# Expert groups recorded as a pipeline, a scatter in two f32r passes, another chain of norms into block 2, a new load price in the plan and an announced branch

## The chip, the core and the metric

The kernel runs on one core of a Trainium2 chip. The metric is the time of one execution on the device in microseconds; the median of three runs is given, and one more execution was taken with the hardware profiler.

## What is computed

Two transformer blocks on 256 tokens of width 1024, all in float32. The first has two kinds of attention and a mixture of experts; the second has two layers, each with a mixer, an attention into 256 memory tokens and a gated feed-forward layer. The change is about the experts and about the passage from the first block to the second:

```python
def hierarchical_moe(h, ...):          # 4 groups x 8 experts, top 2 in the chosen group
    ...
    weight = p_group * softmax(top_vals)
    ...
    def expert_block(args):
        xb, e = args
        return (silu(xb @ w_g[e]) * (xb @ w_u[e])) @ w_d[e]
    ...
    out = zeros((T, D)).at[slot_tok].add(ys * slot_w[:, None])
...
    x = x + hierarchical_moe(rmsnorm(x, ffn_norm), ...)
    return rmsnorm(x, final_norm)      # end of the first block
...
    h = rmsnorm_2(x, norm_mix[0])      # start of the second block
```

There are 32 experts with an inner width of 256, so gate and up weights are 64 MB and down weights 32 MB, all of which are read.

## The kernel before, in words

**Order of the work.** The kernel doesn't issue instructions directly. A `Recorder` (line 164) takes every operation with its tiles; `plan` (line 290) then runs a list schedule over five engines: `price` (line 191) gives each operation a cost, an operation is ready when those it depends on are done and its tiles have a buffer, and of the ready ones an engine takes that with the lowest number (recording order less `bias`). `run` (line 434) then issues everything in the order found, from the one line 461, so nearly all rows name L461. Every engine executes its own instructions strictly in that order. Loads stay in the order of recording on SP's queue; one of 1 MB is priced at 2915 ns (line 221).

**Buffers.** A load of expert weights (`raw`, line 533) is a tile of 8 KB in each partition and takes any free buffer of four shared rings: `w`, `h` and `l` with three each and `n8` with six, less those that operations recorded earlier still need. A slab (`slab`, line 539) for a product in three passes needs one of `w`, `h` and `l`: after the load ACT rounds it to f32r (`h`) and VectorE takes the remainder (`l`), in two halves. A product of two matrices is then three f32r passes, `h` with the high and low part of the other side and `l` with its high part (`mm3`, line 560). Temporary tiles are in the rings `ta` and `tb`, PSUM banks in the rings `pg` (3), `pa` (2), `pb` (2) and `pm` (1).

**The experts' stage** (`moe`, line 1028). Tokens are sorted into 32 slots of each expert by a selection matrix `st`. The loop from line 1048 runs over eight groups of four experts. At each even group the gather (`ga`) of eight experts makes `xs` from f32r parts of x; `cs` is the transposed selection with the routing weights, `rs` the row scale. Each group then has 32 products `gu` (four f32 products of 32 columns side by side, eight loads `w_gu`), the activation `act`, its transposition `at`, 16 products `by` (four loads `w_dn`, in the order first half, second half, first half, second half), two copies `y` on ACT, eight f32 scatter products `co` and four sums into x on VectorE. Then come `MEM_EVERY[g]` steps of the memory (line 1132): 18 steps in all (`memory`, line 1255) make the keys and values of the second block's memory attention, each with one slab `w_xkv` and 48 f32r products `fm` or `tm`. They hold TensorE's time within the stage. One step is in the first block's attention, two run during the routing, 14 in the loop, and one is left and comes behind `two_norms` (line 1554).

Before group 7 two slabs of the second block are recorded, `w_eqk[0]` and `w_ev[0]` (line 1050).

**The branch.** An expert with more than 32 tokens needs more work. It stands behind `tc.If(late > 0)` (line 1149, `moe_late`) and is not taken with these inputs, so each engine jumps over it. The jump comes behind group 1 (`LATEG`), where the plan puts a barrier: only loads are planned across it.

**Into block 2** (`two_norms`, line 1201). Two norms follow one another. The mean of x squared gives `r` by a chain of logarithm, exponential and one Newton step (`rsq`, line 603); a second mean, with the gain, gives `rbc` by a second such chain from the first. The products of the second block take x with both gains before the norm and are multiplied by `rbc` afterwards, so they need not wait for it; `even_mixer` (line 1341) begins with them.

Of the kernel before, what the change touches and what calls it, by code (L numbers as in the profile page):

```python
# [10 lines left out]
F32 = mybir.dt.float32  # L11
# [19 lines left out]
NEXTG = 7  # L31
NEXT = 2
# [5 lines left out]
MEM_EVERY = (2, 2, 2, 2, 2, 2, 1, 1)  # L38
# [125 lines left out]
class Recorder:  # L164
# [5 lines left out]
    TABLE = 1300.0  # L170
    FIRST = "natural_log_exp_and_others"

    def __init__(self, tc, pools):
        self.tc, self.nc, self.pools = tc, tc.nc, pools
        self.count, self.starts, self.bufs, self.ops, self.bars = {}, {}, {}, [], []
        for n in ("tensor", "vector", "scalar", "gpsimd", "sync"):
            setattr(self, n, Engine(self, n))
        self.bias = 0

# [11 lines left out]
    def price(self, engine, method, a, k):  # L191
# [29 lines left out]
        return 2915.0 * n / 2048 if engine == "sync" else 100  # L221
# [212 lines left out]
    def run(self):  # L434
# [13 lines left out]
        for idx, nxt in zip(order, after):  # L448
# [9 lines left out]
    def issue(self, op):  # L458
        r = lambda v: v.real() if isinstance(v, View) else v
        for method, a, k in op.calls:  # L460
            getattr(getattr(self.nc, op.engine), method)(*map(r, a), **{n: r(v) for n, v in k.items()})  # L461


class Net:
# [32 lines left out]
    def consts(self):  # L497
# [25 lines left out]
        self.ones = cp.tile([128, 5, 128], F32, name="ones")  # L523
        for i, v in enumerate((1.0 / 1024, 1.0 / 256, 1.0 / 128, -1.0, 1.0)):
            nc.gpsimd.memset(self.ones[:, i, :], v)
        self.k1024, self.k256, self.k128, self.kneg, self.kone = (self.ones[:, i, :] for i in range(5))
# [3 lines left out]
        for i in range(8):  # L530
            nc.gpsimd.memset(self.order[:, i:i + 1], float(8 - i))

# [70 lines left out]
    def rsq(self, p, out, ms, n, mul=1.0):  # L603
# [4 lines left out]
        nc.scalar.activation(u, ms, AF.Ln, bias=self.eps)  # L608
        nc.scalar.activation(u, u, AF.Exp, scale=-0.5)
        nc.vector.tensor_tensor(t, u, u, ALU.mult)  # L610
        nc.vector.scalar_tensor_tensor(t, ms, EPS, t, ALU.add, ALU.mult)
# [173 lines left out]
    def block1_attention(self, steps):  # L785
# [18 lines left out]
        for i, ac in enumerate(accs):  # L804
            for t in range(2):
                for hf in range(2):
                    o = T * hf + 128 * t
                    self.mm(bs[:, 2 * i + t:2 * i + t + 1], ac[:, o:o + 128], self.kone[:, 0:1], hf == 0, hf == 1)
# [139 lines left out]
    def route(self, rtm):  # L948
# [14 lines left out]
        small = lambda name, *s: self.small(name, 2, *s, bufs=1)  # L963
# [59 lines left out]
        self.mm(b[0:1, 0:1], n, self.kone[:, 0:1])  # L1023
# [4 lines left out]
    def moe(self, steps, early, every):  # L1028
# [17 lines left out]
        slot = self.c("slot")  # L1046
        self.next = []
        for g in range(8):
            if g == NEXTG:
                self.next = [self.slab(w, 256) for w in (a["w_eqk"][0], a["w_ev"][0], a["w_eqk"][1])[:NEXT]]  # L1050
            p, q = divmod(g, 2)
            if q == 0:
                st = self.temp("a", "st", [128, 2, 8, SLOTS], F32R)
                ct, rt = (self.temp("b", n, [128, 2, 8, SLOTS]) for n in ("ct", "rt"))
                for t in range(2):
                    pe = lambda v: v[:, t, 8 * p:8 * p + 8][:, :, None].to_broadcast([128, 8, SLOTS])
                    nc.vector.tensor_tensor(st[:, t], pe(place), slot[:, None, :].to_broadcast([128, 8, SLOTS]),
                                            ALU.is_equal)
                    nc.vector.tensor_tensor(ct[:, t], st[:, t], pe(wt), ALU.mult)
                    nc.vector.tensor_scalar(rt[:, t], st[:, t], rtm[:, t:t + 1], None, ALU.mult)  # L1060
                stv, ctv, rtv = (v.rearrange("p t e s -> p t (e s)") for v in (st, ct, rt))
                xs = self.big("xs", [128, KC, 256])
                for i in range(4):
                    b = self.bank("g", "ga")
                    for j in range(2):
                        c = 2 * i + j
                        for n, (hs, t) in enumerate(((hh, 0), (hl, 0), (hh, 1), (hl, 1))):
                            self.mm(b[:, 256 * j:256 * j + 256], hs[:, t, 128 * c:128 * c + 128], stv[:, t, :],
                                    n == 0, n == 3)
                    for j in range(2):  # L1070
                        c = 2 * i + j
                        gc = self.gcol("ffn_norm", c)
                        if j:
                            nc.scalar.activation(xs[:, c, :], b[:, 256 * j:256 * j + 256], AF.Copy, scale=gc)
                        else:
                            nc.vector.tensor_scalar(xs[:, c, :], b[:, 256 * j:256 * j + 256], gc, None, ALU.mult)
                b = self.bank("m", "cb")
                for i in range(2):
                    for t in range(2):
                        o = 256 * i + 128 * t  # L1080
                        nc.tensor.transpose(b[:, o:o + 128], ctv[:, t, 128 * i:128 * i + 128], self.ident)
                cs = self.temp("b", "cs", [128, 2, T])
                nc.vector.tensor_copy(cs, self.two(b))
                b = self.bank("m", "rs")
                for i in range(2):
                    for t in range(2):
                        self.mm(b[:, i:i + 1], rtv[:, t, 128 * i:128 * i + 128], self.kone[:, 0:1], t == 0, t == 1)
                rs = self.small("rs", 2)
                nc.vector.tensor_copy(rs, b[:, :2])
            bg = self.bank("a", "gu")  # L1090
            for k in range(KC):
                w = self.raw(a["w_gu"][g, k])
                calls = []
                for j in range(4):
                    o = 128 * q + 32 * j
                    calls.append(("matmul", (bg[32 * j:32 * j + 32, :], xs[:, k, o:o + 32],
                                             w[:, 512 * j:512 * j + 512]),
                                  dict(start=k == 0, stop=k == KC - 1, skip_group_check=True)))
                nc.record("tensor", calls)
            act = self.temp("a", "act", [128, 2, 256])  # L1100
            nc.scalar.activation(act[:, 0, :], bg[:, :256], AF.Silu, scale=rs[:, q:q + 1])
            nc.vector.scalar_tensor_tensor(act[:, 0, :], bg[:, 256:], rs[:, q:q + 1], act[:, 0, :],
                                           ALU.mult, ALU.mult)
            b = self.bank("b", "at")
            for i in range(2):
                nc.tensor.transpose(b[:, 128 * i:128 * i + 128], act[:, 0, 128 * i:128 * i + 128], self.ident)
            at = act[:, 1, :]
            nc.vector.tensor_copy(at, b[:, :256])
            by = [self.bank("b", f"by{i}") for i in range(2)]
            for k in range(2):  # L1110
# [579 lines left out]
```

## Time and profile before

| | us |
|---|---|
| median of three runs (1283.58 to 1288.8) | 1283.79 |
| the profiled execution itself | 1278.79 |
| its span in the profile | 1277.0 |
| TensorE busy | 1207.3 |
| VectorE busy | 851.4 |
| ACT busy | 649.5 |

The profile has the busy time of each engine over the whole span and in stretches; TensorE's products are pipelined, so its busy time is not its peak. PE is TensorE, PEld its weight loads, DVE VectorE, ACT ScalarE, POOL GpSimd, SP the queue that issues all loads. An f32 product leaves two records, an f32r product one. The experts' stage lies between about 230 and 515 us.

### The profile page before, as it was taken

What the parts mean: (1) busy time and instruction counts of PE and PEld (TensorE: products, weight loads), DVE (VectorE), ACT (ScalarE), POOL (GpSimd) and SP (SyncE); (2) the same over time, 40 slices, a digit from 0 to 9 for tenths busy, and PEclk for the clock granted to TensorE, in tenths of its full rate; (3) what the DMA queues carried; (4) which work ended last, traced back from release to release, by engine and by line L of the source; (5) the groups of instructions that cost most, each with busy time, mean ns of one, the idle gap of its engine ahead of it and who ended that gap; (6) DMA issues with size and microseconds to landing.
All of it is one profiled execution on the core that took longest, in us unless ns stands there. A gap on an engine that the chain in (4) does not pass through costs nothing.

```text
span 1277.0 us, 22671 instructions
## 1 busy us (share of the span) xinstructions
PE 1207.3 (95%) x9325; PEld 1078.8 (84%) x9325; DVE 851.4 (67%) x1529; ACT 649.5 (51%) x1111; POOL 8.9 (1%) x71
## 2 busy tenths in 40 slices
PE   8999999987878876999999999999999999999998
PEld 7999999555545542898999999999999999999997
DVE  7666677424432242998877977777755687877775
ACT  7664554323322231765545655555766655555543
POOL 1000000000000000000000000000000000000000
PEclk9999999999999998999999999999999999999999
DMA  7623565888999989443441555554433342555541
GB/s 271 238 100 133 214 247 201 340 358 358 392 399 392 420 320 408 164 174 131 167 166 67 198 199 171 193 195 168 166 133 132 106 167 99 192 193 172 185 176 67
DMA packets 40143, 273.55 MB, mean 214 GB/s; under 512 B 4576, under 2 KB 4576, under 8 KB 8032
## 3 DMA queue, kind: packets, MB, share of 16 engines
q1 hardware_dynamic: 40032, 272.03, 57.0%
q8 instruction: 75, 1.23, 0.4%
q14 instruction: 36, 0.29, 0.1%
HBM read 270.96 MB, written 1.05 MB: 213 GB/s over the span
## 4 chain that ended last, share of the span: by engine, by line
PE 67%; DVE 4%; DMA 2%; ACT 2%; issue 1%; SPq 0%; DVEq 0%; ACTq 0%
PE fm L461 41%; PE dn L461 10%; PE tm L461 4%; PE gu L461 2%; DMA w<-w_dn 2%; PE co L461 2%; DVE l L461 2%; PE oz L461 1%; PE by L461 1%; PE mo L461 1%; PE ms L461 1%; PE ga L461 1%; PE hn L461 1%; DMA w<-w_gu 1%; PE bo L461 1%
## 5 line engine op out<-in xcount | busy, mean ns | idle before, releaser
L461 PE MATMUL fm<-xh,h 128*128 128x256 f32 x1824 | 526.9, 290 | 13.9 <-ACT h L461 6.0
L461 PE MATMUL fm<-xh,l 128*128 128x256 f32 x1824 | 518.7, 285 | 6.7 <-DVE l L461 6.7
L461 PE MATMUL fm<-xl,h 128*128 128x256 f32 x1824 | 516.9, 284 | 0.0
L461 DVE TENSOR_TENSOR l<-w,h 128x1024 fp32r<-128x1024 f32 (+2 forms) x328 | 382.9, 1191 | 62.3 <-ACT h L461 61.5
L461 ACT ACTIVATE h<-w 128x1024 fp32r<-128x1024 f32 (+2 forms) x328 | 325.4, 1027 | 178.4 <-issue 86.2
L461 PEld LDWEIGHTS fm<-xh,h 128*128 128x128 f32 x1824 | 350.2, 192 | 18.4 <-ACT h L461 6.9
L461 PEld LDWEIGHTS fm<-xh,l 128*128 128x128 f32 x1824 | 350.5, 192 | 8.3 <-DVE l L461 8.0
L461 PEld LDWEIGHTS fm<-xl,h 128*128 128x128 f32 x1824 | 350.6, 192 | 2.1 <-issue 0.7
L461 PE MATMUL tm<-l,xh 128*128 128x256 f32 (+2 forms) x364 | 104.6, 288 | 3.9 <-DVE l L461 3.9
L461 PE MATMUL tm<-h,xh 128*128 128x256 f32 (+2 forms) x364 | 107.0, 295 | 0.1
L461 PE MATMUL tm<-h,xl 128*128 128x256 f32 (+2 forms) x364 | 104.0, 286 | 0.0
L461 DVE SCALAR_TENSOR_TENSOR fc<-fu,partile,fc 128x256 f32<-128x256 f32 x176 | 73.4, 479 | 1.3 <-ACT fc L461 1.3
L461 PEld LDWEIGHTS tm<-l,xh 128*128 128x128 f32 x364 | 69.6, 191 | 5.2 <-DVE l L461 4.6
L461 PEld LDWEIGHTS tm<-h,xh 128*128 128x128 f32 x364 | 69.4, 191 | 3.0 <-issue 1.3
L461 PE MATMUL gu<-w,xs 128*32 128x512 f32 x512 | 64.9, 623 | 6.3 <-DMA w<-w_gu 6.3
L461 PEld LDWEIGHTS tm<-h,xl 128*128 128x128 f32 x364 | 69.5, 191 | 0.4
L461 PE MATMUL dn<-fa,h 128*128 128x256 f32 x352 | 64.2, 282 | 1.1 <-ACT fa L461 0.6
L461 DVE TENSOR_TENSOR x<-x,co 128x512 f32<-128x512 f32 x32 | 21.8, 687 | 53.6 <-PE co L461 53.6
L461 PE MATMUL dn<-h,fa 128*128 128x512 f32 x176 | 57.0, 396 | 0.0
L461 DVE TENSOR_TENSOR fu<-fm,rbc 128x512 f32<-128x512 f32 x44 | 30.2, 687 | 38.2 <-PE fm L461 38.0
L461 PEld LDWEIGHTS dn<-fa,h 128*128 128x128 f32 x352 | 54.4, 189 | 1.6 <-ACT fa L461 0.8
L461 DVE SCALAR_TENSOR_TENSOR act<-gu,rs,act 128x256 f32<-128x256 f32 x8 | 3.9, 484 | 70.2 <-ACT act L461 70.2
(291 smaller groups left out, 1386.4 us busy)
## 6 DMA issues: line engine op xcount, KB each, us to landing
w<-w_gu SPq DMA_DIRECT2D x64, 1024.0 KB, 8.9
w<-w_up SPq DMA_DIRECT2D x44, 1024.0 KB, 4.9
w<-w_dn SPq DMA_DIRECT2D x32, 1024.0 KB, 9.5
w<-w_down SPq DMA_DIRECT2D x22, 1024.0 KB, 4.9
w<-w_xkv SPq DMA_DIRECT2D x16, 1024.0 KB, 9.6
w<-w_in_d SPq DMA_DIRECT2D x8, 1024.0 KB, 4.8
w<-w_xq SPq DMA_DIRECT2D x8, 1024.0 KB, 4.9
w<-w_xo SPq DMA_DIRECT2D x8, 1024.0 KB, 5.1
```

The lines of the kernel that those rows point to most:

```text
L461: getattr(getattr(self.nc, op.engine), method)(*map(r, a), **{n: r(v) for n, v in k.items()})
```

## The change

- **Pipeline.** The loop is recorded anew: the next group's gate and up products (`gate_up`) stand half behind this group's activation and half behind its first output half; the gather of the next pair (`gather`) stands behind an even group; the output is done in two halves (`expert_out`), each with its own two loads `w_dn`; one memory step stands between the halves, the others at the end. `MEM_EVERY` ends in 0, so 13 steps are in the loop and two are left.
- **Scatter.** The routing weight no longer is in the matrix: `rw` scales the rows of the output, which is split into two f32r parts `yh` and `yl`; the scatter is two f32r passes with the transposed selection `sb` in place of one f32 product.
- **Chain.** `two_norms` sums the squares with and without gain on TensorE and takes `rbc` from both sums in one chain; `r`, for x itself, follows later. `w_eqk[0]` is recorded in group 7 behind all `w_gu`, `w_ev[0]` behind the sums of squares. The two memory steps that are left run behind the products of the first head in `even_mixer`; some keys use other PSUM rings.
- **Plan.** A load of 1 MB is priced at 2480 ns.
- **Branch.** 120 operations ahead of the barrier each engine gets a hint that the jump is likely taken.
- Besides, small tiles are packed: the routing's into one temporary tile, `ones` loses a column block, `ali` uses the ring of `sb`.

```diff
-MEM_EVERY = (2, 2, 2, 2, 2, 2, 1, 1)
+MEM_EVERY = (2, 2, 2, 2, 2, 2, 1, 0)
...
-        return 2915.0 * n / 2048 if engine == "sync" else 100
+        return 2480.0 * n / 2048 if engine == "sync" else 100
...
+        early = [n - self.AHEAD for n, i in enumerate(order) if i < 0]
+        for n, (idx, nxt) in enumerate(zip(order, after)):
+            if n in early:
+                for engine in mybir.ALL_ENGINES:
+                    if engine in self.last:
+                        with tc.issue_after(self.last[engine].ins):
+                            tc.mark_branch_hint_location("late", "LikelyTaken", engines=[engine])
...
+        xs, rest = self.gather(0, hh, hl, place, wt, rtm)
+        banks = [self.bank("a", "gu")]
+        self.gate_up(0, range(KC), xs, banks[0])
         for g in range(8):
...
+            (st, rw), q = rest, g % 2
+            at = self.gated(banks[g], rw, q)
+            if g < 7:
+                if q == 0:
+                    ahead = xs
+                banks.append(self.bank("a", "gu"))
+                self.gate_up(g + 1, range(KC // 2), ahead, banks[g + 1])
+            else:
+                self.next.append(self.slab(a["w_eqk"][0], 256))
+            self.expert_out(g, 0, at, st, rw, q)
+            take = every[g]
+            if take:
+                steps.pop(0)()
+            if g < 7:
+                self.gate_up(g + 1, range(KC // 2, KC), ahead, banks[g + 1])
+            self.expert_out(g, 1, at, st, rw, q)
+            if g % 2 == 0 and g < 6:
+                ahead, later = self.gather(g // 2 + 1, hh, hl, place, wt, rtm)
+            if q:
+                xs = ahead
+                if g < 7:
+                    rest = later
             if g == LATEG:
                 nc.barrier(lambda: self.moe_late(hh, hl, rtm, wlate, flag), [hh, hl, rtm, wlate, flag, x])
-            for _ in range(every[g]):
+            for _ in range(max(0, take - 1)):
                 steps.pop(0)()
...
+    def expert_out(self, g, i, at, sb, rw, q):
...
+        yh, yl = (self.temp(p, n, [128, 512], F32R) for p, n in (("a", "yh"), ("b", "yl")))
+        self.parts(yh, yl, by, rw[:, 2 + q:3 + q])
+        for h in range(2):
+            b = self.bank("g", "co")
+            for j in range(2):
+                s = slice(256 * h + 128 * j, 256 * h + 128 * j + 128)
+                self.mm(b[:, T * j:T * j + T], yh[:, s], sb[:, q, :], True, False)
+                self.mm(b[:, T * j:T * j + T], yl[:, s], sb[:, q, :], False, True)
+            xv = x[:, 4 * i + 2 * h:4 * i + 2 * h + 2, :]
+            nc.vector.tensor_tensor(xv, xv, self.two(b), ALU.add)
...
-        with tc.If(late > 0):
+        with tc.If(late > 0, label="late"):
...
+        acc = self.tile([128, 512], "acc", "acc", 2)
+        b = self.bank("m", "st")
         for i in range(4):
+            sq = self.temp("s", "sq", [128, 512])
             for c in (2 * i, 2 * i + 1):
                 self.parts(xh[:, c, :], xl[:, c, :], x[:, c, :], gg[:, c:c + 1])
...
+            nc.scalar.activation(sq, self.pair(x, i), AF.Square)
             for j in range(2):
...
+                self.mm(b[:, :T], self.k1024, sq[:, s], i == 0 and j == 0, False)
+                if i:
+                    nc.vector.scalar_tensor_tensor(acc[:, s], sq[:, s], g, acc[:, s], ALU.mult, ALU.add)
...
+        nc.vector.tensor_scalar(ms, b[:, :T], EPS, EPS * EPS, ALU.mult, ALU.add)
+        nc.vector.tensor_tensor(ms, ms, b[:, T:], ALU.add)
+        self.rsq("s", rbc, ms, T, eps=0.0)
+        self.next.append(self.slab(self.a["w_ev"][0], 256))
         nc.bias = -LATER
+        self.rsq("s", r, b[:, :T], T)
...
+            if hd == 0:
+                while steps:
+                    steps.pop(0)()
```

## Rows read from the trace of the kernel before

**Rows 1.** The page's busy times: us, share of the span, instructions.

```profile
PE 1207.3 (95%) x9325; PEld 1078.8 (84%) x9325; DVE 851.4 (67%) x1529; ACT 649.5 (51%) x1111; POOL 8.9 (1%) x71
```

**Rows 2.** Table of stretches: length, busy time of each engine, clock, transfers' share, GB/s.

```profile
280.00:290.00 10.00, 5.97 (x39) 4.29 (x37) 4.42 (x6) 4.38 (x5) 0.00 (x0) 1.00 0.58 211
...
300.00:305.00 5.00, 5.00 (x40) 4.95 (x41) 2.07 (x4) 2.40 (x3) 0.00 (x0) 1.00 0.61 197
...
315.00:325.00 10.00, 7.34 (x70) 2.62 (x62) 3.68 (x11) 2.30 (x4) 0.00 (x0) 1.00 0.70 270
325.00:360.00 35.00, 28.12 (x204) 18.68 (x200) 19.82 (x40) 12.50 (x21) 0.00 (x0) 0.95 1.01 420
360.00:365.00 5.00, 3.37 (x30) 0.88 (x26) 0.94 (x3) 0.47 (x1) 0.00 (x0) 1.00 0.85 324
...
390.00:395.00 5.00, 3.37 (x34) 0.88 (x26) 0.91 (x2) 0.47 (x1) 0.00 (x0) 1.00 0.77 293
...
455.00:460.00 5.00, 5.00 (x45) 3.24 (x47) 3.53 (x9) 1.40 (x4) 0.00 (x0) 1.00 0.76 267
...
470.00:480.00 10.00, 7.00 (x41) 5.20 (x42) 5.72 (x7) 6.83 (x8) 0.00 (x0) 1.00 0.58 206
...
515.00:545.00 30.00, 29.85 (x232) 28.47 (x231) 29.84 (x60) 22.92 (x39) 0.00 (x0) 1.00 0.40 145
```

**Rows 3.** TensorE's timeline at the stage's end: start, us, instruction, idle time before it.

```profile
493.00 1.07 PE L461 MATMUL gu<-w,xs 128*32 128x512 f32 x8 [1.42 <-DMA w<-w_gu]
495.50 1.94 PE L461 MATMUL gu<-w,xs 128*32 128x512 f32 x8 [1.44 <-DMA w<-w_gu]
497.99 1.93 PE L461 MATMUL gu<-w,xs 128*32 128x512 f32 x8 [0.55 <-DMA w<-w_gu]
...
507.96 1.06 PE L461 MATMUL by<-w,act 128*32 128x512 f32 x8 [1.33 <-DMA w<-w_dn]
...
515.74 0.39 PE L461 MATMUL fm<-xh,h 128*128 128x256 f32 x1
```

**Rows 4.** Instructions of the branch's line: durations ns min/median/max, first and last start us.

```profile
L1149 SPq EVENT_SEMAPHORE  x8: 17/17/17, 279.0 to 285.2; - x8
...
L1149 SPq COMPARE_BRANCH  x1: 50/50/50, 273.6 to 273.6; - x1
...
L1149 PEldq COMPARE_BRANCH  x1: 6252/6252/6252, 286.7 to 286.7; - x1
```

**Rows 5.** Waits on SP and on TensorE in 265 to 330: us, times, longest.

```profile
SPq L461 <- DVE hn_sq L461: 12.6, 1, 12.6
...
PE fm L461 <- PEq L1149: 4.7, 1, 4.7
```

**Rows 6.** SP's timeline from 455: start, us of issuing, loads.

```profile
463.38 0.33 SPq L461 DMA_DIRECT2D w<-w_eqk  x1
469.95 0.33 SPq L461 DMA_DIRECT2D w<-w_ev  x1
...
502.18 0.33 SPq L461 DMA_DIRECT2D w<-w_xkv  x1
```

**Rows 7.** The chain that ended last, pieces from 306 to 526: start, us, what.

```profile
306.17 2.83 PE ga L461 x24
...
326.45 0.61 ACT y L461
327.10 1.99 PE co L461 x8
...
383.53 7.05 PE gu L461 x64
...
525.59 0.43 PE st L461 x2
```

**Rows 8.** Groups of VectorE in 230 to 517: busy us, mean ns, idle before them.

```profile
L461 DVE TENSOR_TENSOR l<-w,h 128x1024 fp32r<-128x1024 f32 x29 | 33.8, 1218 | 3.2 <-ACT h L461 3.2
L461 DVE TENSOR_TENSOR x<-x,co 128x512 f32<-128x512 f32 x32 | 21.8, 687 | 53.6 <-PE co L461 53.6
```

More of the change, by code (lines that the diff above doesn't have):

```diff
@@ L178, in __init__ @@
         self.bias = 0
+        self.last = {}
     def tile(self, shape, dtype, name, tag=None, bufs=1, space="sb"):
@@ L531, in consts @@
             nc.gpsimd.memset(self.order[:, i:i + 1], float(8 - i))
+        self.kone = self.order[:, 7:8]
     def raw(self, ap):
@@ new lines, in gate_up @@
+    def gate_up(self, g, ks, xs, bg):
+        for k in ks:
+            w = self.raw(self.a["w_gu"][g, k])
+            calls = []
+            for j in range(4):
+                o = 128 * (g % 2) + 32 * j
+                calls.append(("matmul", (bg[32 * j:32 * j + 32, :], xs[:, k, o:o + 32],
+                                         w[:, 512 * j:512 * j + 512]),
+                              dict(start=k == 0, stop=k == KC - 1, skip_group_check=True)))
+            self.rec.record("tensor", calls)
@@ new lines, in gated @@
+    def gated(self, bg, rw, q):
+        nc = self.rec
+        act = self.temp("a", "act", [128, 2, 256])
+        nc.scalar.activation(act[:, 0, :], bg[:, :256], AF.Silu, scale=rw[:, q:q + 1])
+        nc.vector.scalar_tensor_tensor(act[:, 0, :], bg[:, 256:], rw[:, q:q + 1], act[:, 0, :],
+                                       ALU.mult, ALU.mult)
+        b = self.bank("b", "at")
+        for i in range(2):
+            nc.tensor.transpose(b[:, 128 * i:128 * i + 128], act[:, 0, 128 * i:128 * i + 128], self.ident)
+        at = act[:, 1, :]
+        nc.vector.tensor_copy(at, b[:, :256])
+        return at
@@ L1175, in moe_late @@
                 ac = tile([128, 2, T], "ac", "tb")
-                bu = [bank("pa", f"lu{i}") for i in range(2)]
+                bu = [bank("pg", f"lu{i}") for i in range(2)]
                 for k in range(KC):
@@ L1231, in two_norms, with head_norm @@
         return (xh, xl), rbc
-    def head_norm(self, p, b, ones, pairs, rbc, out, gains, mul=1.0):
+    def head_norm(self, p, b, ones, pairs, rbc, out, gains, mul=1.0, bank=None):
         nc = self.rec
@@ L1284, in keys @@
         def keys(l, s):
-            b = self.fm(self.slab(a[f"w_xkv{l}"][s], 256), state["x"])
+            b = self.fm(self.slab(a[f"w_xkv{l}"][s], 256), state["x"], tag="b" if l and s > 1 else "g")
             self.head_norm("ab"[s % 2], b, self.k256, True, state["r"], self.mem_k[l][:, s],
-                           [self.gcol(f"xk{l}", j) for j in range(2)])
+                           [self.gcol(f"xk{l}", j) for j in range(2)], bank="m")
         def values(l, s):
@@ L1339, in mem_attention, with even_mixer @@
         self.project(a[f"w_xo{l}"], ox)
-    def even_mixer(self, x, rbc):
+    def even_mixer(self, x, rbc, steps):
         nc, a = self.rec, self.a
@@ L1366, in even_mixer @@
             b = self.fm(self.next.pop(0) if self.next else self.slab(a["w_eqk"][hd], 256), x)
+            if hd % 2 == 0:
+                w = self.next.pop(0) if self.next else self.slab(a["w_ev"][hd // 2], 256)
+                bs = self.by_token_products(w, x)
             qk = self.temp(p, "eqk", [128, 2, T])
@@ L1369, in even_mixer @@
             if hd % 2 == 0:
-                w = self.next.pop(0) if self.next else self.slab(a["w_ev"][hd // 2], 256)
-                bs = self.by_token_products(w, x)
                 for t in range(2):
@@ L1553, in record @@
         x, rbc = self.two_norms()
-        while steps:
-            steps.pop(0)()
         for l in range(2):
@@ L1559, in record @@
             else:
-                self.even_mixer(x, rbc)
+                self.even_mixer(x, rbc, steps)
             self.mem_attention(l)
```

193 lines of the change are left out of this document (82 added, 111 removed).

## The prediction

> **What bounds the kernel now.** The page first: TensorE is busy for 1207.3 of 1277.0 us [rows 1], so most of the program is bound there and only a stretch with other limits can give much. The table of stretches, read from the start of the experts' stage to the head of block 2, shows such a stretch. From 230 us to about 510 us the transfers run at a share of 1.00 or more and some 420 GB/s, in seven places excepted [rows 2]. In 515 to 545 us it is the other way round: TensorE is busy 29.85 and VectorE 29.84 of 30 us, the transfers 0.40 [rows 2]. So the stage's length is its bytes at full rate plus the gaps in the transfers, and what TensorE does in it is worth nothing unless it makes a gap. The last group proves it: its gate and up products start 2.49 to 2.50 us apart, each released by its own load [rows 3], and that is what one load of 1 MB takes.
>
> The gaps are the prize. Share short of 1, times length [rows 2]: 280 to 290, 4.2 us; 300 to 305, 1.95; 315 to 325, 3.0; 360 to 365, 0.75; 390 to 395, 1.15; 455 to 460, 1.2; 470 to 480, 4.2. Together 16.45 us, 1.3% of the run. Three causes can be read off.
>
> At the branch, SP took its own jump at 273.6 us, yet stood at the branch's semaphores until 285.2 us [rows 4]; its issued loads ran out meanwhile, which is the first gap. TensorE's jump took 6252 ns [rows 4] and its next products waited 4.7 us for it [rows 5]. VectorE, in order, stood behind those products, so a slab's split was late, and SP stood 12.6 us for that part of VectorE's queue [rows 5]: the gap at 300. At 463 to 470 us two slabs for block 2 (`w_eqk`, `w_ev`) are issued ahead of group 7's weights [rows 6]; their buffers hold SP, and that is the gap at 470. The others stand where a group ends: TensorE waits for ACT's copies, does the eight scatter products and then two memory steps in a row, while full buffers wait.
>
> **The change, part by part.** The sum is made on the profiled execution (1278.79 us, of which 1277.0 span) and then laid on the median of the runs, 1283.79, which is 5 us above it; I take the difference as equal in both.
>
> *Pipeline over groups.* No product is added or taken in gate, up and down. Half of the next group's gate and up products (four times 0.89, from one group's 7.05 us [rows 7]) come behind the activation, half behind the first output half; one memory step stands between instead of two at the end. So buffers are freed more evenly. The gaps at 315, 360, 390 and 455 sum to 6.1 us; I take two thirds, **4.0**, because buffers are no more numerous: `y` leaves the large buffers, but a second `xs` lives there in its stead. On SP's queue four loads of the next group now pass ahead of this group's `w_dn`, so those land up to 4 x 2.5 us later in the order; the four gate and up products that use the earlier ones are the cover, and a saturated queue loses nothing by order alone. POOL's queue is not touched.
>
> *Loads for block 2.* `w_ev` goes behind group 7's last load: one load out of the stage, **2.5 us** [rows 3]. Transfers have room behind it (0.40 [rows 2]). `w_eqk` stays ahead of the last four loads but behind all of `w_gu`. So the two slabs no longer hold SP at 470: of 4.2 us I take **3.0**. The memory step that moves behind the first head costs nothing here, since its load was already issued at 502.18 us, behind the last `w_dn` [rows 6].
>
> *Branch announced.* If it works, TensorE's 4.7 us go and with them the gap at 300: **1.95**. The gap of 4.2 at 280 stays, since SP waits there for the other engines, not for its fetch. [...]
>
> *Scatter.* 64 products at 1.99 us for four (two records each [rows 7]) are 31.8 us; 128 f32r products at the gather's price, 2.83 us for 24 [rows 7], are 15.1. The 16.7 us lie beside saturated transfers and count as 0, but for the last half group. New are 16 splits: ACT's part costs what the copy did (0.61 [rows 7]), VectorE's some 0.69 (a 512 wide operation from PSUM [rows 8]), 11 us in all, where VectorE is far from full; 0.
>
> *Last half group.* Before, from the third `w_dn` released at 507.96 to the first product of block 2 at 515.74 [rows 3]; the fourth load lands about 2.5 later, 510.5, and 5.1 us of halves follow. After: down 1.06, ACT 0.61, VectorE 0.69, two scatters 0.47 each, so some 2.9 to 3.3 us. Gain **2.2**. Behind it stands the sum into x (0.69) and the split of the last chunks, while the first chunks' products run.
>
> *Another chain.* Nine sums of squares over TensorE in place of two, at 0.43 [rows 7]: +3.0 us, half of it while loads are awaited, so **+1.5**. One square-root chain (two ACT and four VectorE operations) leaves the way to `rbc`, but TensorE has slabs to work on meanwhile and idles 0.15 us in 515 to 545 [rows 2]: 0. VectorE loses two sum chains but has `w_ev`'s split to do there, 2 x 1.22 [rows 8]; about even, up to +2.4 if it isn't.
>
> *New load price.* The plan took 2.915 us, takes 2.48; the rows have 2.49 to 2.50 [rows 3]. It moves orders everywhere, also in the stages bound by TensorE; 0, with 3 us either way.
>
> *Sum*: -4.0 - 2.5 - 3.0 - 1.95 - 2.2 + 1.5 = -12.2 us; 1283.8 - 12.2 = **1271.6 us**.
>
> **The rivals.** About 0.5%, 6.4 us, is what a measurement of this kernel can tell from no change.
>
> *The gaps only move.* Buffers, not the order, set when a load goes out: same number of buffers, SP strictly in order, slabs still holding three each. For it: the long waits of SP are for buffers [rows 5]. Against it: the gaps stand at the groups' ends and at the branch, not evenly. Then only `w_ev`, the tail and the sums count: -2.5 - 2.2 + 1.5, **1280.6 us**, chance 0.18.
>
> *The announcement does nothing.* The jump stays at 6.25 us, and with it the gap at 300 and some of the one at 315: +3, **1274.6 us**, chance 0.06.
>
> *The new price is too low.* Where a load takes longer than the plan thinks, TensorE's queue is headed by products whose weights are not there, while a memory step that could run stands behind them. By the rows the error is at most 2.50 - 2.48 = 0.02 us a load [rows 3], 12 loads in each of eight groups, 1.9 us: 1273.5 us, chance 0.02. [...]
>
> *VectorE's queue in front of the splits.* Sixteen new `yl` wait on `w_dn` through ACT; on VectorE, in order, the slabs' splits that free load buffers stand behind them, as one stood behind `hn_raw` at 300 [rows 5]. Thirteen slabs are split in the stage; each split 1.3 us later (0.61 + 0.69) with no buffer to cover it is 16.9 us, and no gap comes back: 1280.6 + 16.9 = **1297.5 us**. It decides from 12.2 / 13 = 0.94 us a slab. Against it: the sum into x waited in the same place already, and VectorE is idle 53.6 us before it [rows 8]. Chance 0.09.
>
> **How the numbers follow.** The forecast has 0.65; its own range is 1263 to 1278. With the announcement failing and the low price, faster has 0.73; the moved gaps are the 0.18 of no change; VectorE's queue is the 0.09 of slower. The low end takes all gaps but the one at 280 (12.25), 2.5, 2.2 and 3 for the plan, and counts the sums as 0: 1283.8 - 20 = 1264, and 1260 if the branch's gap closes too. The high end, 1284, takes no gap, `w_ev` alone, and +2.4 for VectorE. The slower rival is left out.
>
> **What would show it.** Right: shares of 0.95 or more from 305 to the end of the loads; the last `w_dn` about 11 us earlier; TensorE's jump under 1 us; no wait of 12 us on SP behind VectorE; a third of the way from the last load to block 2's products gone. Wrong: the same idle total of transfers at other places (gaps moved); SP's waits for VectorE's `l` longer than now (the slower rival); or TensorE idle in the 30 us behind the last sum into x, which would mean that one ready slab in place of two, and VectorE, are the new limit and that what the stage gives is handed back there.

## The result, and the profile after

The changed kernel takes 1276.68 us (median of 17 executions, 1272.71 to 1280.38), the kernel before 1281.86 in the same comparison (17 executions): ratio 0.9949, 95% interval 0.9935 to 0.9962. By this ratio, which the text goes by, that is 6.5 us less (the two medians lie 5.2 apart): just past what a measurement can tell from no change, and half of the 12.2 forecast. The profiled execution took 1273.56 us, 1271.8 of it span; like the profiled one of the kernel before (1278.79) it lies 3.1 us under its median, so the two can be set side by side.

Cut at the same landmarks (first gather product, end of the last sum into x, the mixer's first sum into x, end), the two profiled executions differ so:

| stretch | before | after | |
|---|---|---|---|
| up to the experts' stage | 230.6 | 230.4 | -0.2 |
| stage, to the last sum into x | 285.9 | 275.6 | -10.3 |
| from there to the mixer's first sum | 109.6 | 116.0 | +6.4 |
| the rest | 651.0 | 649.8 | -1.2 |

So the stage gave 10.3 us, and the even mixer of block 2 handed 6.4 of them back.

The page's busy times of the kernel after, which answer [rows 1]:

```profile
PE 1213.5 (95%) x9371; PEld 1084.3 (85%) x9371; DVE 861.4 (68%) x1546; ACT 648.0 (51%) x1103; POOL 9.0 (1%) x70
```

VectorE has 10 us more and TensorE 6 us more than before, though f32r products were to make TensorE's work less (the run with the f32 scatter, below, comes back to this). The table of stretches of the kernel after (length, busy time of PE, PEld, DVE, ACT, POOL, granted clock, transfers' share, GB/s), which answers [rows 2]:

```profile
280.00:290.00 10.00, 8.91 (x76) 4.67 (x75) 0.75 (x1) 2.78 (x5) 0.00 (x0) 1.00 1.00 395
300.00:305.00 5.00, 4.95 (x41) 2.18 (x43) 1.27 (x3) 1.52 (x3) 0.00 (x0) 1.00 1.02 421
305.00:315.00 10.00, 5.82 (x44) 2.18 (x36) 5.48 (x12) 5.13 (x6) 0.00 (x0) 1.00 0.59 220
315.00:325.00 10.00, 9.95 (x82) 6.59 (x80) 3.16 (x4) 1.70 (x3) 0.00 (x0) 1.00 1.01 422
...
360.00:365.00 5.00, 5.00 (x44) 1.80 (x46) 4.52 (x11) 4.50 (x11) 0.00 (x0) 1.00 1.01 416
390.00:395.00 5.00, 3.90 (x35) 1.28 (x28) 1.00 (x3) 1.73 (x3) 0.00 (x0) 1.00 1.01 419
455.00:460.00 5.00, 5.00 (x37) 3.60 (x30) 0.33 (x2) 0.00 (x0) 0.00 (x0) 0.85 1.01 416
470.00:480.00 10.00, 8.44 (x66) 6.49 (x67) 4.91 (x7) 2.45 (x3) 0.00 (x0) 1.00 0.79 304
```

The gaps at 300, 315, 360, 390 and 455 are gone, the one at 470 is half as long (2.1 us), and the one at the branch stays (4.1 us, now at 305 to 315). The branch's line after, answering [rows 4]: TensorE's jump is 392 ns in place of 6252, while SP still stands at its semaphores, up to 308.5 us.

```profile
L1206 SPq EVENT_SEMAPHORE  x8: 17/17/17, 300.1 to 308.5; - x8
...
L1206 PEldq COMPARE_BRANCH  x1: 392/392/392, 308.9 to 308.9; - x1
```

The stage no longer ends with its loads. SP's timeline before,

```profile
488.98 8.85 SPq L461 DMA_DIRECT2D w<-w_dn  x4
```

and after, answering [rows 6]: the last `w_dn` is issued by 482.34 us, 15.5 earlier than before, and behind it only `w_ev`.

```profile
475.11 0.42 SPq L469 DMA_DIRECT2D w<-w_eqk  x1
475.63 6.71 SPq L469 DMA_DIRECT2D w<-w_dn  x4
485.48 0.33 SPq L469 DMA_DIRECT2D w<-w_ev  x1
```

What ends it is VectorE's timeline (start, us, instruction, idle time before it):

```profile
485.96 0.48 DVE L469 SCALAR_TENSOR_TENSOR act<-gu,rw,act 128x256 f32<-128x256 f32 x1 [3.15 <-ACT act L469]
...
492.84 2.35 DVE L469 TENSOR_TENSOR l<-w,h 128x1024 fp32r<-128x1024 f32 x2
495.11 0.74 DVE L469 SCALAR_TENSOR_TENSOR yl<-by,rw,yh 128x512 fp32r<-128x512 f32 x1
...
503.18 0.75 DVE L469 SCALAR_TENSOR_TENSOR yl<-by,rw,yh 128x512 fp32r<-128x512 f32 x1 [2.23 <-ACT yh L469]
504.68 1.29 DVE L469 TENSOR_TENSOR x<-x,co 128x512 f32<-128x512 f32 x2 [0.75 <-PE co L469]
```

The split of `w_eqk` (2.35 us) stands ahead of `yl`, and TensorE waited 2.24 us for that `yl`:

```profile
495.91 0.39 PE L469 MATMUL co<-sb,yl 128*128 128x256 f32 x1 [2.24 <-DVE yl L469]
```

From the end of group 7's act (486.44) to the last sum (505.97) it takes 19.5 us, against 13.3 before. This is not `yl` alone: TensorE's timeline has eight records of the sums of squares and twelve products of block 2 ahead of the last scatter there, and before none. Counted from the first gather product, group 7's act comes 16.6 us earlier than before, and this tail takes 6.2 of them back.

And the 6.4 us handed back: TensorE's timeline and the stretches there. TensorE stands 5.77 us behind VectorE's `cu`, and then runs 5 us with the clock at 0.69.

```profile
590.00 0.58 PE L469 MATMUL fm<-xh,h 128*128 128x256 f32 x1 [5.77 <-DVE cu L469]
```

```profile
585.00:590.00 5.00, 0.00 (x0) 0.00 (x0) 5.00 (x18) 2.26 (x10) 0.10 (x1) 0.62 0.15 29
590.00:595.00 5.00, 5.00 (x31) 5.00 (x31) 3.58 (x10) 0.91 (x2) 0.00 (x0) 0.69 0.44 184
```

### The profile page after: what moved, and what is told of

Read it like the earlier page. It is cut to its first block, busy times and chain, and to the rows that moved or that the text cites. A ratio compares the mean times of both kernels' runs of the same rounds, so it can differ in the third digit from the quotient of the medians.

```text
span 1271.8 us, 22754 instructions
## 1 busy us (share of the span) xinstructions
PE 1213.5 (95%) x9371; PEld 1084.3 (85%) x9371; DVE 861.4 (68%) x1546; ACT 648.0 (51%) x1103; POOL 9.0 (1%) x70
## 4 chain that ended last, share of the span: by engine, by line
PE 67%; DVE 5%; DMA 2%; ACT 1%; issue 0%; SPq 0%; ACTq 0%
PE fm L469 42%; PE dn L469 10%; PE tm L469 4%; PE gu L469 2%; PE oz L469 1%; DVE l L469 1%; PE mo L469 1%; PE ms L469 1%; DMA w<-w_gu 1%; PE by L469 1%; DMA w<-w_xkv 1%; PE hn L469 1%; DVE x L469 1%; PE bo L469 1%; PE st L469 1%; PE ga L469 0%
## 5 line engine op out<-in xcount | busy, mean ns | idle before, releaser
L469 DVE SCALAR_TENSOR_TENSOR yl<-by,rw,yh 128x512 fp32r<-128x512 f32 x16 | 12.0, 749 | 55.7 <-ACT yh L469 55.7
L469 PE MATMUL dn<-fa,l 128*128 128x256 f32 x176 | 49.6, 282 | 0.0
```

The source lines that it names most:

```text
L469: self.last[engine.engine] = getattr(engine, method)(*map(r, a), **{n: r(v) for n, v in k.items()})
```

## The experiments

All twelve in one table, the profiled execution cut as above ("stage": first gather product to the last sum into x; "mixer": from there to the mixer's first sum), with the median and the ratio to the kernel before, which ran beside each. The variants did not run beside the changed kernel, so what a part is worth is a difference of two such ratios, uncertain by some 3 us either way. "Stage" and "mixer" are of one execution each: "convolution first" has the changed kernel's order up to the last sum into x, and yet a stage 3.0 us longer.

| kernel | stage | mixer | median us | ratio (95%) |
|---|---|---|---|---|
| before | 285.9 | 109.6 | 1281.9 to 1284.2 | 1 |
| changed | 275.6 | 116.0 | 1276.68 | 0.9949 (0.9935 to 0.9962) |
| changed, no announcement | 282.0 | 116.0 | 1282.98 | 1.0003 (0.9982 to 1.0024) |
| before, announcement alone | 287.9 | 111.1 | 1278.76 | 0.9962 (0.9944 to 0.9981) |
| changed, old price | 284.0 | 117.9 | 1285.77 | 1.0013 (0.9992 to 1.0034) |
| before, new price alone | 285.7 | 115.4 | 1283.96 | 1.0001 (0.9984 to 1.0018) |
| changed, f32 scatter | 268.7 | 114.3 | 1268.63 | 0.9885 (0.9860 to 0.9911) |
| changed, old chain | 278.0 | 124.2 | 1287.46 | 1.0027 (1.0008 to 1.0046) |
| changed, `w_eqk` last | 276.8 | 122.8 | 1282.69 | 0.9986 (0.9966 to 1.0006) |
| changed, step in stage | 289.3 | 110.0 | 1283.24 | 0.9979 (0.9959 to 1.0000) |
| changed, steps first | 275.6 | 116.1 | 1278.27 | 0.9967 (0.9948 to 0.9987) |
| changed, convolution first | 278.6 | 113.6 | 1277.08 | 0.9956 (0.9935 to 0.9976) |
| changed, idle products | 287.4 | 115.9 | 1287.25 | 1.0036 (1.0019 to 1.0053) |
| both of the last two | 292.1 | 113.6 | 1285.74 | 1.0016 (1.0004 to 1.0028) |

**The announcement, taken out of the changed kernel.**

```diff
-        early = [n - self.AHEAD for n, i in enumerate(order) if i < 0]
+        early = []
```

> The changed kernel without the announcement of the branch. Theory (the announcement frees TensorE at the branch, and the stage bound by transfers passes on a part of it): TensorE's jump is back at about 6 us instead of 0.39, a gap in the transfers comes back behind the branch, and the last sum into x lies 2 to 4 us later than 506; total 1 to 4 us above the changed kernel. Rival (the stage is bound by transfers and buffers are full of loads at the branch, so the jump is covered): last sum within 1 us of 506, total the same.

The whole gain goes, 0.0054 of the time or 6.9 us, more than the theory had. The jump is long again, though not 6 us:

```profile
L1206 PEldq COMPARE_BRANCH  x1: 3592/3592/3592, 309.6 to 309.6; - x1
```

The order of the work is the same; at group 2's act only 0.9 us have been lost, counted from the first gather product, at the last sum 6.4. The rest arises behind it, where TensorE's clock falls (0.77 over 310 to 325 and over 470 to 485) and a gap in the transfers follows (share 0.63 over 470 to 485). Whether each execution without the announcement falls there, one trace doesn't show.

**The announcement alone, put into the kernel before** (the same loop, 120 operations ahead, and the label of the branch).

> The kernel before with nothing but the announcement of the branch (120 operations ahead). Theory A (the jump is worth what the transfers stood for it): TensorE's jump falls from 6.25 us to about 0.4 us, the gap of the transfers at 300 us (1.95 us) closes, and the time falls by 1 to 2.5 us (ratio 0.998 to 0.999). Theory B (the announcement is worth what its removal cost the changed kernel, some 6 us, whatever surrounds it): ratio 0.995 to 0.996. Theory C (in the old order the loads catch up before the stage ends): no change, ratio 1.000.

0.0038 of 1283.2 us, **4.9 us** (2.4 to 7.2 by the interval): more than the gap of 1.95. Branch and stretches of this kernel, to set beside [rows 2, 4]:

```profile
L1157 PEldq COMPARE_BRANCH  x1: 392/392/392, 287.0 to 287.0; - x1
```

```profile
300.00:305.00 5.00, 4.99 (x35) 3.75 (x34) 4.89 (x13) 2.38 (x4) 0.00 (x0) 1.00 1.02 426
315.00:325.00 10.00, 7.65 (x54) 2.82 (x50) 1.59 (x3) 2.35 (x3) 0.00 (x0) 0.91 1.00 383
...
355.00:360.00 5.00, 5.00 (x23) 1.93 (x23) 0.16 (x1) 0.00 (x0) 0.00 (x0) 0.50 0.58 210
```

Both the gap at 300 and the one at 315 are gone, 1.95 + 3.0 = 4.95 us. So the second was not, as the prediction had it, the end of a group alone: with the same order of work it goes with the jump. But that these two gaps are the 4.9 us is not shown. In this trace the loss has moved: at 355 to 360 the clock is 0.50 and the share 0.58, where before it was 1.01, and in slices of 5 us from 245 to 500 the shares short of 1 sum to 17.0 us against 17.5 before. (This profiled execution was the longest of its ten, 1281.1 us of span against 1274.1 to 1278.0, so its stage of 287.9 is not typical. No trace of a typical one exists.)

**The old price in the changed kernel, and the new price alone in the old one.**

```diff
-        return 2480.0 * n / 2048 if engine == "sync" else 100
+        return 2915.0 * n / 2048 if engine == "sync" else 100
```

> The changed kernel with the old load price of 2915 ns in the plan. Theory (the price only shifts orders; the pipeline closes the gaps): last sum into x at 506 to 510, total within 3 us of the changed kernel either way. Rival (the price is what made the plan fit the transfers): the gaps of 16 us are back for the most part, last sum at 512 or later, total 5 us above the changed kernel or more.

> The kernel before with nothing but the plan's price of a 1 MB load at 2480 ns in place of 2915. Theory A (the price is worth something only where the order leaves the plan a choice, as in the pipelined stage, where the old price cost 9 us): within 3 us of before, ratio 0.998 to 1.002, gaps of the transfers still at the ends of the groups. Theory B (the price alone brings the gain, and the pipeline little): ratio 0.993 to 0.996.

In the kernel before, the price does nothing for the time (1.0001), as the first theory said. In the changed one the old price costs 0.0064, 8.2 us, as its rival said: transfers at a share of 0.59 over 360 to 370 and 0.64 over 485 to 510 in its stretches. That a price matters where the order leaves the plan a choice fits both runs. But it moves orders elsewhere too: with the new price alone the mixer takes 115.4 us in place of 109.6, and TensorE waits there for `cu` longer. Before,

```profile
PE fm L461 <- DVE cu L461: 2.4, 2, 2.1
```

and with the new price alone (us, times, longest):

```profile
PE fm L461 <- DVE cu L461: 5.8, 2, 4.6
```

**The scatter of before in the changed kernel.** One f32 product for two f32r passes, no `yl`; the weight stays on the rows of the output:

```diff
-        yh, yl = (self.temp(p, n, [128, 512], F32R) for p, n in (("a", "yh"), ("b", "yl")))
-        self.parts(yh, yl, by, rw[:, 2 + q:3 + q])
+        y = self.temp("a", "yh", [128, 512])
+        nc.scalar.activation(y, by, AF.Copy, scale=rw[:, 2 + q:3 + q])
...
-                self.mm(b[:, T * j:T * j + T], yh[:, s], sb[:, q, :], True, False)
-                self.mm(b[:, T * j:T * j + T], yl[:, s], sb[:, q, :], False, True)
+                self.mm(b[:, T * j:T * j + T], y[:, s], sb[:, q, :])
```

> The changed kernel with the scatter of before: y scaled by the weight on ScalarE alone, one f32 product in place of two f32r passes, no yl on VectorE (16 x 0.75 = 12.0 us less there), TensorE's product longer (0.38 us a record against 0.28). Theory A (my term for the scatter, 0: both hide under the transfers): ratio 0.993 to 0.997, the last sum into x within 2 us of the changed kernel's by the time since group 7's act (19.5 us). Theory B (yl behind the split of w_eqk is what holds up the tail): group 7's act to the last sum 15 to 17.5 us, ratio 0.990 to 0.993. Theory C (any other order of the stage brings back the falls of the clock at 310 to 325 and 470 to 490 us): act of group 7 at 489 us or later, ratio 0.997 to 1.003.

Better than any theory had it: **1268.63 us**, 0.9885, some 8.2 us less than the changed kernel and 14.8 less than before. The intervals don't overlap. This version beats both. The table of stretches, of the kernel before:

```profile
230.00:516.40 286.40, 230.91 (x1688) 143.40 (x1687) 101.88 (x180) 87.75 (x129) 0.00 (x0) 0.97 0.94 381
516.40:626.10 109.70, 106.97 (x848) 101.91 (x847) 100.36 (x218) 64.14 (x126) 0.40 (x4) 1.00 0.41 145
```

of the changed kernel:

```profile
230.00:506.00 276.00, 237.28 (x1744) 148.83 (x1743) 113.83 (x209) 88.50 (x129) 0.00 (x0) 0.94 0.96 392
506.00:622.00 116.00, 108.51 (x846) 103.21 (x845) 99.67 (x214) 61.35 (x118) 0.51 (x4) 0.97 0.42 146
```

and of the one with the f32 scatter:

```profile
230.00:499.60 269.60, 237.68 (x1734) 147.76 (x1733) 103.58 (x194) 88.81 (x130) 0.00 (x0) 0.97 0.98 402
499.60:613.90 114.30, 109.82 (x850) 104.64 (x850) 100.44 (x214) 60.62 (x118) 0.40 (x4) 0.97 0.42 147
...
470.00:480.00 10.00, 9.09 (x75) 6.27 (x71) 1.80 (x4) 1.96 (x3) 0.00 (x0) 1.00 1.01 417
480.00:495.00 15.00, 11.74 (x72) 5.04 (x64) 10.79 (x22) 9.90 (x15) 0.00 (x0) 1.00 1.01 418
```

TensorE is busy equally long in the last two stages, 237.3 and 237.7 us, although its scatter records are shorter with f32r (281 ns against 379) and are busy for 23.6 us in place of 31.9. The granted clock differs: 0.94 against 0.97. In the changed kernel's trace the clock is 0.50 over 330.2 to 337 us and 1.00 over 593 to 600, with no level between, and f32r products of one shape follow one another 0.21 us apart at 0.50 (591 to 592.5) and 0.12 at 1.00 (594 to 595). By an estimate from these two levels a mean of 0.94 means 2 x 0.06 x 276 = 33 us at the lower, 0.97 means 16; the 17 us more at half speed are some 8 us of work. So the lower clock takes about what the shorter products save. This is a sum of sizes; why the clock is lower, it doesn't show. VectorE has 12 us of `yl` on top:

```profile
L469 DVE SCALAR_TENSOR_TENSOR yl<-by,rw,yh 128x512 fp32r<-128x512 f32 x16 | 12.0, 749 | 55.7 <-ACT yh L469 55.7
```

SP, too, waits longer. Its longest waits between 230 and 500 us (us, times, longest), changed kernel:

```profile
SPq L469 <- PE gu L469: 78.0, 44, 8.7
SPq L469 <- DVE l L469: 63.3, 10, 8.9
```

and with the f32 scatter:

```profile
SPq L469 <- PE gu L469: 65.5, 43, 7.1
SPq L469 <- DVE l L469: 47.9, 10, 7.7
```

In the kernel before, SP waited 30.4 us there for VectorE's `l`; the change doubled that, and about half of the growth goes with `yl`. Without `yl` the transfers run full up to 495 us but for the branch's gap, group 7's act comes 4.2 us earlier (counted from the first gather product), and from the act to the last sum takes 16.9 us in place of 19.5, as the second theory expected. Of the 6.9 us that the stage is shorter, the gaps in the transfers make 2.3 (6.2 against 3.9) and the tail 2.6; the rest has no single place. The plan also makes another order of it, so this is the scatter and what the plan makes of it, not `yl` alone: VectorE's queue, the clock and the order weren't told apart.

**The old chain into block 2 in the changed kernel** (`two_norms` as before, with `w_ev`'s slab at the changed place).

> The changed kernel with the old chain into block 2 (two sums of squares on VectorE, two means, a root of the product), the slab of w_ev recorded where the changed kernel has it. Theory A (my term: the new chain costs 0 to 2.4 us on VectorE): last sum into x to the mixer's first sum 114 to 116 us (116.0 in the changed kernel), ratio to before 0.993 to 0.995. Theory B (the new chain is shorter where it counts, between the last sum into x and the first norm of the mixer, and hides the tail): that stretch 118 us or more, ratio 0.996 to 0.999.

The second theory, and beyond its range: 8.2 us more in the mixer (124.2), 0.0078 on the ratio. TensorE's wait for `hn_raw` there is new, beside that for `cu`:

```profile
PE fm L469 <- DVE cu L469: 4.7, 2, 4.4
PE fm L469 <- DVE hn_raw L469: 4.7, 2, 3.7
```

`hn_raw` is what needs `rbc`. So the chain's length does count in the changed order, and the new one is a gain there, not a cost. In the old order the same chain stands in a mixer of 109.6 us; a run of the new chain in that order is missing.

**`w_eqk` behind group 7's outputs**, to clear the tail of its split.

```diff
-            else:
-                self.next.append(self.slab(a["w_eqk"][0], 256))
...
             self.expert_out(g, 1, at, st, rw, q)
+            if g == 7:
+                self.next.append(self.slab(a["w_eqk"][0], 256))
```

> The changed kernel with the first w_eqk slab recorded behind group 7's two outputs, not ahead of them. Theory A (the split of w_eqk on VectorE, 2.35 us, stands ahead of the last yl and holds up the tail of the stage): group 7's act to the last sum into x falls from 19.5 us to 16 to 17.5, and the ratio to before to 0.992 to 0.994 if the mixer keeps its 116 us. Theory B (what the tail gains, the first product of the mixer gives back, since its slab is then split later): tail shorter by 2 to 3 us, the stretch to the mixer's first sum longer by as much, ratio 0.994 to 0.996.

Second theory, and worse than even: the act is followed by the last sum within 16.1 us, but the mixer takes 122.8. What this run is worth most for is that TensorE's order up to group 7's outputs is that of the changed kernel, and yet the stage runs differently. Its stretches,

```profile
312.50:322.50 10.00, 8.09 (x41) 6.00 (x42) 3.20 (x4) 3.20 (x3) 0.00 (x0) 0.66 1.01 417
470.00:475.00 5.00, 3.95 (x18) 0.78 (x18) 2.87 (x7) 2.92 (x4) 0.00 (x0) 0.66 0.98 408
475.00:480.00 5.00, 3.79 (x29) 2.82 (x30) 4.31 (x5) 2.11 (x3) 0.00 (x0) 1.00 0.04 16
```

and the same of the changed kernel:

```profile
312.50:322.50 10.00, 8.21 (x66) 6.50 (x70) 3.65 (x5) 3.09 (x3) 0.00 (x0) 1.00 1.01 419
470.00:475.00 5.00, 3.44 (x26) 2.46 (x27) 4.82 (x7) 2.45 (x3) 0.00 (x0) 1.00 0.73 301
475.00:480.00 5.00, 5.00 (x42) 4.03 (x42) 0.09 (x1) 0.00 (x0) 0.00 (x0) 1.00 0.85 306
```

Two falls of the clock, behind the branch and behind group 6's act, and the act of group 7 stands at 490.09 in place of 485.45 us, with the same start (230.3 and 230.4).

**One memory step back in the stage** (`MEM_EVERY` ending in 1).

> The changed kernel with one memory step in group 7 as before (MEM_EVERY ends in 1), so that one fewer is left for the mixer. Theory A (the 6.3 us handed back in the mixer are the work of the step that the change moved there): the stretch from the last sum into x to the mixer's first sum falls from 116.0 to 110 to 112 us, the last sum into x comes 2 to 4 us later, ratio 0.992 to 0.996. Theory B (the mixer is bound by VectorE's order, whatever step is left): the stretch stays at 114 to 118 us, the last sum comes later by the load of one more slab (2.5 us) or more, ratio 0.996 to 1.000.

The mixer takes 110.0 us, the first theory's number, but not for its reason. Stretch and wait, to set beside the changed kernel's:

```profile
521.00:631.00 110.00, 101.28 (x776) 95.87 (x775) 91.58 (x202) 55.26 (x111) 0.40 (x4) 0.97 0.36 127
```

```profile
PE fm L469 <- DVE cu L469: 6.6, 2, 5.4
```

TensorE has 70 records and 7.2 us of work less in the mixer, since these run in the stage now; the wait for `cu` stays at 6.6 us, against 7.0 in the changed kernel and 2.4 before. And before, the mixer did 848 records in 109.6 us, as many as the 846 that take 116.0 in the changed kernel. So of the 6.4 us the longer wait is 4.6, and TensorE is busy 1.5 us longer for as much work, at a clock of 0.97 against 1.00; taking the step back doesn't remove the wait. The new price alone brings most of it in the kernel before (5.8). With the old price in the changed kernel it is 4.1 us, but the mixer is no shorter (117.9). What makes VectorE come late to `cu` stays open.

The stage pays 13.7 us for the step in place of the 2 to 4 expected, 2.6 ahead of group 7's act and 11.1 behind it, where the step's products stand. So the change's place for it is the better one.

**Steps first, and convolution first**, two ways to free VectorE's queue in the mixer: the leftover memory steps right behind `two_norms`, or `cr`, `cu` and the first `cy` put forward by 400 places.

> The changed kernel with the two last memory steps recorded before the heads of block 2, as before the change, instead of behind the first head. Theory (the 6.3 us that the stretch from the last sum into x to the first sum behind the mixer grew come from the memory steps between the heads, which push the heads' chain and the convolutions together): TensorE's wait of 5.8 us for VectorE's cu falls under 3 us, the stretch goes from 116 to 110 to 112, total 3 to 6 us below the changed kernel. Rival (the wait comes from the order on VectorE at the convolutions whatever stands before the heads): the wait stays at 4 us or more and the total within 2 us.

> The changed kernel with the three operations that free the convolutions' PSUM banks (cr, cu, first cy) ahead of the last head's operations in the plan's priority. Theory (TensorE stands 5.8 us because these wait in VectorE's queue behind the last head): wait under 3 us, total 3 to 5 us below the changed kernel. Rival (they become ready late in the plan's own time, so their priority does not move them in the queue): wait as now, total within 1.5 us.

Neither is worth anything that can be told. The first leaves the mixer at 116.1 and the longest wait for `cu` at 4.3, as its rival said; the second takes 2.4 us off the mixer and the longest wait from 5.8 to 5.4 only, with the total as its rival said.

**Idle products on TensorE**, in its waits for `act`, to see whether the granted clock stays up there; alone and with the convolution first:

```diff
+        if hasattr(op, "fill"):
+            for _ in range(7):
+                engine.matmul(*map(r, op.fill), start=True, stop=True, skip_group_check=True)
```

> The changed kernel, its order of work as it is, with seven idle products (128x128 f32 into an unused half of the bank of `at`) on TensorE ahead of each group's first transpose of act, where it waits some 1.9 us for act; they leave the results as they are. [...]

> The same idle products, with the mixer's cr, cu and first cy put forward by 400 places as in the run that did that alone (its stretch from the last sum into x to the mixer's first sum was 113.5 us against 116.0). Theory A (the two effects add up): the stage as with the idle products alone, the mixer's stretch 113 to 114 us, ratio 0.988 to 0.992. Theory B (the mixer's stretch is ruled by the clock behind its own wait, not by the order): the stretch 115 to 117 us, ratio as with the idle products alone.

Both lost time: 0.0087 and 0.0067 worse than the changed kernel. The second's first theory had a ratio of 0.988 to 0.992 (its mixer, 113.6 us, came as that theory said). The clock did stay at 1.00 behind the branch, but it was lower later, and over the stage 0.93 against 0.94. Stretches with the idle products,

```profile
310.00:325.00 15.00, 13.55 (x106) 8.84 (x106) 5.45 (x8) 5.68 (x6) 0.00 (x0) 1.00 0.93 376
435.00:445.00 10.00, 7.60 (x34) 5.11 (x35) 4.31 (x5) 2.30 (x3) 0.00 (x0) 0.66 1.00 408
...
475.00:490.00 15.00, 12.72 (x74) 6.66 (x75) 7.18 (x12) 4.89 (x6) 0.00 (x0) 0.77 0.54 212
```

and of the changed kernel:

```profile
435.00:445.00 10.00, 9.77 (x68) 6.94 (x72) 1.31 (x2) 0.95 (x2) 0.00 (x0) 0.83 1.02 422
...
475.00:490.00 15.00, 11.92 (x90) 6.79 (x90) 3.36 (x8) 7.85 (x10) 0.00 (x0) 1.00 0.96 386
```

In the last of these the transfers' share is 0.54 against 0.96, at a clock of 0.77 against 1.00. That a low clock and late loads go together is seen here and in the run of `w_eqk` last (clock 0.66 over 470 to 475, share 0.04 over 475 to 480); which of them leads is not shown, nor that filling TensorE's waits raises the clock.

## Why the prediction was right, and where not

The direction and the range held; the size was 12.2 us and came out as 6.5. By the prediction's own steps:

- *What bounds the stage*: right for the gaps, not for the stage's end. The gaps fell from 16.45 us to 6.2 (4.1 and 2.1), and the last `w_dn` is issued 15.5 us earlier, where the signs had about 11. But the stage is only 10.3 shorter, because in the changed kernel its loads no longer end it.
- *Pipeline, 4.0, and loads for block 2, 2.5 and 3.0*: in the profiled execution the gaps at 360, 390 and 455 are gone and the one at 470 halved, of which the announcement alone took neither 390 nor 455 to 480, and the price alone not 455 to 480. Not told apart by a run of its own: the pipeline without the other parts wasn't tried, so its share is argued.
- *Branch announced, 1.95*: mis-sized. It is **4.9 us** alone in the kernel before, and its removal costs 6.9 in the changed one. The gap at 315 (3.0), which the pipeline's term counted, closes with the announcement alone. Where the 4.9 us come from the trace doesn't say, since its closed gaps come back elsewhere. The gap at the branch stays, as the step said.
- *Scatter, 0*: **this step failed.** It costs 8.2 us, by the run that takes it back. TensorE's part was mis-sized (128 passes are busy for 23.6 us, not 15.1). The prediction looked for cover and found the transfers, but `yl` stands in VectorE's queue, in order, between one product and the next: TensorE waits 2.24 us for one in the tail, where the stage no longer waits for its loads. The rival of VectorE's queue named such a mechanism, and the sign that it gave (longer waits of SP for `l`: 30.4 us in the stage, then 63.3) came true; but they are still 47.9 without `yl`, and the transfers' gaps are only 2.3 of the 6.9 us that the stage gets shorter. So the cost is shown, that it arises in VectorE's queue only in part. The rival was priced at twice the cost (16.9), and given 0.09.
- *Last half group, 2.2*: failed. The tail from group 7's act grew from 13.3 to 19.5 us; without `yl` it is 16.9, with `w_eqk` behind it 16.1. By its own rows the step's gain was 1.8 to 2.2 (5.1 less 2.9 to 3.3), and it counted one half group alone, while the plan puts `w_eqk`'s split, the sums of squares and products of block 2 among the last halves.
- *Another chain, +1.5*: wrong sign in the changed order, where the old one costs some 10 us more (1.0027 against 0.9949). That TensorE "has slabs to work on meanwhile" holds with the new chain (busy 29.63 of the 30 us from 506); with the old one it waits 4.7 us for `hn_raw`.
- *The memory step moved, 0*: its load was early, as the step said, and the 6.4 us lost in the mixer are not shown to be its work. They are for the most part a longer wait for `cu`, with TensorE busy longer at a lower clock; the wait stays when the step goes back, and comes with the new price alone. The prediction's last sign of error, TensorE idle behind the last sum into x, came 78 us behind that sum, not within 30.
- *New price, 0 with 3 either way*: right for the time of the kernel before (1.0001), though its mixer is 5.8 us longer in the trace; in the pipeline the price is worth 8.2. For the rival of a price too low nothing speaks: the transfers of the changed kernel run at 419 GB/s over 318 to 445 us, where before it was 420 over 325 to 360, and of the two prices tried in it that near 2.5 us is the better one.

That the time came out within the range is partly luck. (The ends worked out there are 1260 and 1284, the range is given as 1263 to 1278; 1276.68 lies in both.) Cut at the same landmarks, the profiled executions say where the forecast went. Up to group 7's act 16.6 us were gained, where pipeline, loads and branch were put at 11.45. From there to the last sum 6.2 were lost, where 2.2 were to be gained. The mixer lost 6.4, where the chain was to cost 1.5. With 1.3 gained outside, that is 5.3 us in place of 12.2: more was gained ahead than forecast, and much more lost behind.

## What to carry to other kernels

Before calling an added instruction covered by transfers, look on the queue in which it stands for a buffer's release or a stage's end that waits for it: here TensorE waited 2.24 us for a `yl` in the tail, where the loads no longer end the stage. Try an announcement where a branch stands in the middle of a saturated stage: here it was worth 4.9 us alone and 6.9 in the changed kernel. When a gap closes, sum the gaps of the whole stage before taking it as gain: here they came back elsewhere in the one trace (17.0 us against 17.5). And take parts of a bundle back one by one: here the best version was the bundle less one part. Look in each such run at the wait itself, not only at the length: a stretch got shorter by the expected 6 us while the wait that it was meant to remove stayed.

## What the hardware showed

- TensorE's jump is long where it isn't announced: it took 6.25, 3.80 and 3.59 us in the three kernels without the announcement and 0.39 or 0.40 in the eleven with it. What the long one waits for, the traces don't show; the page of the kernel before counts 75 packets on the instruction queue q8, those of the changed kernel and of the one with the f32 scatter 74.
- The same program runs the same order at different granted clocks. Of the changed kernel's 17 executions, nine with a mean clock of 0.985 to 0.987 have spans of 1270.9 to 1274.9 us, eight with 0.978 to 0.981 have 1275.7 to 1278.6. With the f32 scatter the clock is 0.990 to 0.992 in all five. With seven idle products in TensorE's waits the clock was lower, not higher, in stretches from 435 to 490 us (0.66 against 0.83 over 435 to 445, 0.77 against 1.00 over 475 to 490). Why one execution falls at 312 us and another of the same order doesn't, after nearly the same standstill (TensorE busy 1.32 and 1.20 us of 310 to 312.5), stays open.
